# Split key, value and query weights of layer one stored by its second batch, cached rows written back from loaded tiles, and a new order of the work

## The chip, the cores and the metric

The kernel runs on one core of a Trainium2 chip. The metric is the device time of one launch in microseconds. Lower is better. Before the change the median of three runs is 2243.28 us (2240.95 to 2246.43).

## What is computed

Two layers of a streaming encoder on float32 data. There are 1024 frames of one new stream and 16 frames of each of eight running streams, 1152 rows of 1024 columns together. Each layer is a mixer and a gated convolution network, both added to the input:

```python
def trunk_layer(x, pos, cache_k, cache_v, ...):
    xn = rms_norm(x, norm_mix)
    q, k, v, u = mixer_inputs(xn, pos, w_in, q_gain, k_gain)     # xn @ w_in, 512 | 128 | 128 | 512 columns
    if cache_k is None:                                          # the new stream: a band of key chunks
        attn = window_attention_prompt(q, k, v, sinks); keys, vals = k, v
    else:                                                        # running streams: 128 cached keys and 16 new ones
        keys = jnp.concatenate([cache_k, k], axis=1); vals = jnp.concatenate([cache_v, v], axis=1)
        attn = sink_attention(q, keys, vals, sinks, None)
    pool, new_pool = pool_mixer(u, pool_prev, w_pool, pool_scale)
    x = x + jnp.concatenate([attn, pool], axis=-1) @ w_out
    f, new_conv = conv_ffn(rms_norm(x, norm_ffn), conv_prev, w_up, conv_w, conv_b, w_down)
    return x + f, keys[:, -WINDOW:], vals[:, -WINDOW:], new_pool, new_conv
```

The new cache of a running stream holds the 128 newest rows: rows 16 to 127 of the old cache, then the 16 new ones.

## The kernel before

**Tiles and batches.** The 1152 rows are nine tiles of 128 (tile 8 holds the running streams), in three batches of three tiles. A mixer works batch by batch. `n` streams normalise a batch and transpose it for TensorE. `k` units (12 in a batch) multiply it with the query, key and value columns of `w_in`, `u` units (8) with the pooling columns, `p` units (4) with the pooling weights, and `o` units (16) with `w_out`. A chain of steps named `L` prepares the heads and attends, tile after tile, in one fixed order. Then `m` streams normalise again, `s` units form the sums and differences of blocks for a Strassen product, and the up projection starts with units `v` (first half of the rows) and `w` (second half) on weights that `up_advance` loads and splits (`upw` does it ahead). The first up products are followed by a long regular stage (`up_units`), and that by the down projection in seven products (`down_units`, j from 0 to 6, with p counting the tiles of one product).

**Split weights.** A product is made of three matmuls on rounded parts (`mm3`): high by high, high by low, low by high. A piece of weights of 256 KB is loaded into a `raw` tile (5 buffers), ScalarE or VectorE rounds it into the high part, and VectorE subtracts to get the low part, both in one `W` tile (6 buffers, 512 KB). `w_split` (line 173) does this and, where the piece has a key, stores the split tile in DRAM (`wsd`, lines 187 to 189). A later unit with the same key finds it in `kept` and loads the split tile back with one 512 KB transfer (lines 178 to 180) and neither load nor split of its own. Three later splits and up to five later raw loads are written ahead of a unit (`w_advance`). So each mixer's first batch loads, splits and stores, and the second and third batches load the stored tiles. `keyed` (line 1359) gives the keys.

**The caches.** `sample` loads `cache_k` and `cache_v` of a layer as tiles of 128 partitions (cached row) by 8 streams by 128 (`load`, line 666; `loadv`, line 670). Rows 16 to 127 go to the output apart from that, DRAM to DRAM, in `copies` (line 1338), a unit that waits for nothing.

**Order.** Each unit is a `Token` with a key from `PLAN`: a stream has a first key and a step. `arrange` sorts by key and puts out the first unit whose predecessors are out and whose tiles have room. That is the order in which instructions are written. The framework then orders each queue again: instructions keep their written rank, and one that waits for nothing can be moved forward past others that do. All data transfers are issued by SyncE (SP), whose queue runs in order: a transfer that waits holds up those behind it. The DVE, ACT and PE queues run in order too.

**Other places the change touches.** `params1` (unit `par`) has 12 small transfers: two gains, the sinks nine times, and the pooling scale into a tile of the tag `D`. `xl1` loads the three input tiles of the second batch. `wt_load` (called in `down_units`, line 1221) loads six pieces of `w_down` into `W` tiles, one in each of p = 0 to 3 and two at p = 4 of the first down product; the third down product is the first to use them. Flags in `PLAN` (`e_...`) say for some copies whether VectorE (1) or ScalarE (0) makes them.

Of the kernel before, what the change touches and what calls it, by code (L numbers as in the profile page):

```python
# [44 lines left out]
def arrange(tokens, limits):  # L45
# [17 lines left out]


PLAN = [
    dict(k0=(-17.62, 0.24), u0=(10.61, 1.71), k1=(30.79, 2.26), u1=(78.0, 4.62), o0=(92.76, 2.89), k2=(148.67, 0.53), u2=(167.09, 2.77), o1=(177.0, 4.18), o2=(235.82, 4.28), p0=(40.1, 4.11), p1=(87.53, 9.52), p2=(194.05, 11.9), n1=(-17.77, 3.16), n2=(24.42, 3.62), n3=(92.75, 0.67), m0=(218.99, 3.57), m1=(259.62, 0.1), m2=(181.18, 1.22), d=(4.13, 4.36), L=(26.9, 49.72, 64.52, 85.1, 108.8, 144.29, 159.45, 183.94, 209.44, 245.41), cw=(276.93, 6.24), sc=(242.61, 32.45), s0=(252.65, 2.67), s1=(279.21, 6.7), v=(236.08, 0.18), w=(265.61, 1.32), upw=(297.57, 0.58), e_q=0, e_k=1, e_v=1, e_u=0, e_k2=0, e_qt=0, e_pt0=0, e_pt1=1, e_ps0=1, e_ps1=1, e_ks=0, e_w=1, e_x0=0, e_x1=0, e_x2=1),
    dict(k0=(-52.3, 0.11), u0=(39.12, 0.62), k1=(27.74, 4.1), u1=(77.36, 4.61), o0=(81.16, 2.69), k2=(144.54, 0.53), u2=(154.52, 4.44), o1=(176.58, 5.19), o2=(244.07, 2.25), p0=(50.25, 5.11), p1=(72.82, 0.77), p2=(195.1, 13.29), n1=(-13.38, 2.12), n2=(30.2, 4.39), n3=(93.86, 2.01), m0=(219.6, 1.94), m1=(237.49, 1.8), m2=(278.02, 1.14), d=(-26.81, 5.35), L=(26.9, 49.72, 64.52, 87.91, 107.72, 142.58, 160.43, 180.13, 216.19, 239.71), cw=(266.26, 12.19), sc=(271.63, 4.65), s0=(264.1, 2.05), s1=(266.18, 3.7), v=(283.58, 0.14), w=(284.07, 11.47), upw=(287.29, 0.87), e_q=1, e_k=1, e_v=0, e_u=1, e_k2=0, e_qt=0, e_pt0=0, e_pt1=0, e_ps0=1, e_ps1=1, e_ks=0, e_w=1, e_x0=0, e_x1=1, e_x2=0),
]


# [1 line left out]
def encoder_kernel(ctx: ExitStack, tc: tile.TileContext, consts, x_prompt, x_sample, cache_k, cache_v,  # L72
# [4 lines left out]
    pe, act, dve, pool, sync = nc.tensor, nc.scalar, nc.vector, nc.gpsimd, nc.sync  # L77
# [14 lines left out]
    def T(tag, shape, dt=F32):  # L92
        cnt[0] += 1
        n = 1
        for s in shape[1:]:
            n *= s
        assert n <= SIZE[tag], (tag, shape)
        t = sp.tile([128, SIZE[tag]], dt, tag=tag, name=f"{tag}{cnt[0]}", bufs=BUFS[tag])
        v = t[0:shape[0], 0:n]
        if len(shape) == 3:  # L100
            v = v.rearrange("p (a b) -> p a b", b=shape[2])
        elif len(shape) == 4:
            v = v.rearrange("p (a b c) -> p a b c", b=shape[2], c=shape[3])
        return v
# [556 lines left out]
    def sample(l):  # L661
        H = {}
# [3 lines left out]
        def load():  # L666
            H["ck"] = T("B", [128, 8, 128])
            sync.dma_start(out=H["ck"], in_=cache_k[l].rearrange("b t g d -> t b (g d)"))

        def loadv():  # L670
            H["cv"] = T("B", [128, 8, 128])
            sync.dma_start(out=H["cv"], in_=cache_v[l].rearrange("b t g d -> t b (g d)"))

        def kc(i):
            def f():
# [522 lines left out]
    def down_units(l):  # L1198
        us = []
        for u, (j, p) in enumerate(DSEQ):  # L1200
            n = 5 if j in (0, 1, 5, 6) else 4
            late = j == 5 and l < DEPTH - 1
            loads, splits = ((0, 2, 4, 5, 6), (0, 0, 2, 4, 5)) if n == 5 else ((0, 2, 4, 6), (0, 0, 2, 4))

            def f(u=u, j=j, p=p, n=n, late=late, loads=loads, splits=splits):
                if u == 0:
                    down_x(l, 0)
                if u + 2 < len(DSEQ):
                    g_load(l, u + 2)
                if u + 1 < len(DSEQ):  # L1210
                    down_x(l, u + 1)
                    g_split(l, u + 1)
                down_add(l, u, None)
                if j < 6 and not late:
                    for x in range(*(splits + (6,))[p:p + 2]):
                        wd_split(l, j + 1, x)
                    for x in range(*(loads + (6,))[p:p + 2]):
                        wd_load(l, j + 1, x)
                if j == 0:
                    for x in range(p, 6 if p == 4 else p + 1):  # L1220
                        wt_load(l, x)
# [12 lines left out]
            us.append(Unit(f))  # L1234
        return us

# [8 lines left out]
    def params1(l):  # L1245
        def f():
# [88 lines left out]
        x_load(0, [1, 2])()  # L1335
        sync.dma_start(out=cst[:, C_M:C_END], in_=consts[:, C_M:C_END])

    def copies(l):
        def f():
            sync.dma_start(out=nk_s[l, :, 0:112], in_=cache_k[l, :, 16:128])  # L1340
            sync.dma_start(out=nv_s[l, :, 0:112], in_=cache_v[l, :, 16:128])
        return f

    events = []
    pend = []
    for l in range(DEPTH):
# [9 lines left out]
                q = list((pre or {}).get(i, ())) + ([f"{st}.{i - 1}"] if i else [])  # L1356
                add(f"{st}.{i}", k + i * step, u, q, (res or {}).get(i))

        def keyed(x, units, l=l):
            for i, u in enumerate(units):  # L1360
                u.ws[0].key = l, x, i
            return units
# [24 lines left out]
            first = {3 if wd else 1: {"T6": 6}} if sn[0] == "n" else {}  # L1387
            stream(sn, norms(l, ts, sn[0], normB if sn[0] == "n" else normQ, wd), {0: npre[sn]}, first)
        add("spl", pl["u2"][0] - 20, spool_load(l), ["k1.11"])
        add("copy", pl["o1"][0], copies(l))  # L1390
        for b in range(3):
            nn = f"n{b + 1}.5"
            kres = {7: {"qkv": 3}, 11: {"V": 3}}
            stream(f"k{b}", keyed("k", kvq_units(l, b)), {0: [nn] + ([f"k{b - 1}.11"] if b else []), 11: ["par"]}, kres)
            stream(f"u{b}", keyed("u", u_units(l, b)), {0: [nn] + (["d.9"] if l else []), 3: [f"p{b - 1}.3"] if b else [], 7: [f"p{b}.0"] + (["spl"] if b == 2 else [])}, {7: {"T6": -6}})
# [14 lines left out]
            add(f"L.{i}", key, f, ([f"L.{i - 1}"] if i else ["par"] + (["d.9"] if l else [])) + list(pre), res)  # L1410
            lastidx[t] = i
        for b in range(3):
            ou = keyed("o", out_units(l, b))
# [93 lines left out]
```

## Time and profile before

| | |
|---|---|
| median of the runs | 2243.28 us |
| profiled execution, its own time | 2242.44 us |
| its span, first to last instruction | 2240.7 us |
| mean granted TensorE clock | 0.988 of 2.4 GHz |
| busy PE / DVE / ACT / POOL | 97% / 76% / 42% / 15% |
| chain that ended last: PE / DMA / DVE / ACT | 85% / 6% / 5% / 2% |
| moved by DMA | 389.64 MB, mean 174 GB/s |

The numbers come from one execution. The outside of the span is 1.7 us. A row of busy time says how long an engine had an instruction in work. Matmuls overlap, so their durations add up to more than the time they take; the starts of two neighbours give the real pace. The granted clock is 1.00 at 2.4 GHz and 0.5 at 1.2 GHz; a value between is a mean over a stretch with both. The mixer of layer one runs from 0 to about 405 us, its up projection to about 885 us, its down projection into layer two's mixer, which ends at about 1505 us; layer two's up projection ends at about 1985 us.

### The profile page before, as it was taken

What the parts mean: (1) busy time and instruction counts of PE and PEld (TensorE: products, weight loads), DVE (VectorE), ACT (ScalarE), POOL (GpSimd) and SP (SyncE); (2) the same over time, 40 slices, a digit from 0 to 9 for tenths busy, and PEclk for the clock granted to TensorE, in tenths of its full rate; (3) what the DMA queues carried; (4) which work ended last, traced back from release to release, by engine and by line L of the source; (5) the groups of instructions that cost most, each with busy time, mean ns of one, the idle gap of its engine ahead of it and who ended that gap; (6) DMA issues with size and microseconds to landing.
All of it is one profiled execution on the core that took longest, in us unless ns stands there. A gap on an engine that the chain in (4) does not pass through costs nothing.

```text
span 2240.7 us, 36002 instructions
## 1 busy us (share of the span) xinstructions
PE 2169.5 (97%) x13178; PEld 1945.5 (87%) x13178; DVE 1712.6 (76%) x3234; ACT 943.5 (42%) x1749; POOL 326.6 (15%) x499
## 2 busy tenths in 40 slices
PE   7999999899999999999999999979999999999999
PEld 6867777899999999878888887779999999988887
DVE  4776467989899998867557754689989999987663
ACT  3454345534343434443335543554343434353341
POOL 0000001121213232000000000111212233320000
PEclk9999999899999999999999999999999999999999
DMA  8757565122224346958765665532222343488663
GB/s 313 255 194 269 182 218 173 59 95 79 95 88 151 117 151 220 298 178 268 243 228 184 230 230 207 205 116 84 94 82 93 110 140 128 143 274 267 182 199 113
DMA packets 315940, 389.64 MB, mean 174 GB/s; under 512 B 21906, under 2 KB 219746, under 8 KB 315730
## 3 DMA queue, kind: packets, MB, share of 16 engines
q1 hardware_dynamic: 315762, 387.33, 52.2%
q8 instruction: 104, 1.70, 0.3%
q14 instruction: 74, 0.61, 0.1%
HBM read 279.71 MB, written 109.37 MB: 174 GB/s over the span
## 4 chain that ended last, share of the span: by engine, by line
PE 85%; DMA 6%; DVE 5%; ACT 2%; issue 1%; SPq 0%; POOL 0%; DVEq 0%; ACTq 0%
PE mm L154 15%; PE mm L155 15%; PE mm L156 15%; PE s L156 11%; PE s L154 11%; PE s L155 11%; PE s L644 2%; DMA raw<-in_w_down_dram 1%; DMA raw<-in_w_in_dram 1%; PE tr L631 1%; PE mm L448 1%; DMA W<-wd1o 1%; PE s L592 1%; DMA xd<-u 1%; PE tr L294 1%
## 5 line engine op out<-in xcount | busy, mean ns | idle before, releaser
L154 PE MATMUL mm<-B,W 128*128 128x288 f32 (+1 forms) x1376 | 422.1, 307 | 13.6 <-DVE B L927 7.7
L155 PE MATMUL mm<-B,W 128*128 128x288 f32 (+1 forms) x1376 | 419.2, 305 | 1.9 <-DVE B L315 1.8
L156 PE MATMUL mm<-B,W 128*128 128x288 f32 (+1 forms) x1376 | 417.2, 304 | 0.0
L154 PE MATMUL s<-B,B 128*128 128x512 f32 x704 | 279.6, 397 | 4.1 <-ACT B L1133 2.7
L156 PE MATMUL s<-B,B 128*128 128x512 f32 x704 | 279.2, 397 | 2.8 <-DVE B L1134 2.8
L155 PE MATMUL s<-B,B 128*128 128x512 f32 x704 | 278.6, 396 | 0.0
L154 PEld LDWEIGHTS mm<-B,W 128*128 128x128 f32 x1376 | 262.6, 191 | 17.9 <-DVE B L927 7.9
L155 PEld LDWEIGHTS mm<-B,W 128*128 128x128 f32 x1376 | 262.0, 190 | 3.4 <-DVE B L315 2.4
L156 PEld LDWEIGHTS mm<-B,W 128*128 128x128 f32 x1376 | 261.7, 190 | 1.0 <-DVE W L185 0.4
L975 DVE SCALAR_TENSOR_TENSOR B<-B,cvp,B 128x1168 f32<-128x1168 f32 x176 | 250.6, 1427 | 1.8 <-ACT B L973 1.5
L154 PE MATMUL mm<-W,B 128*128 128x512 f32 (+1 forms) x576 | 220.0, 388 | 12.4 <-ACT W L184 3.1
L155 PE MATMUL mm<-W,B 128*128 128x512 f32 (+1 forms) x576 | 214.8, 374 | 0.2 <-DVE W L185 0.2
L156 PE MATMUL mm<-W,B 128*128 128x512 f32 (+1 forms) x576 | 213.9, 374 | 0.0
L868 ACT CAST W<-Q 128x512 fp32r<-128x512 f32 x132 | 82.0, 621 | 258.1 <-PE mm L156 169.3
L1133 ACT CAST B<-B 128x256 fp32r<-128x256 f32 (+1 forms) x128 | 97.3, 780 | 204.7 <-DMA B<-gd 70.5
L154 PE MATMUL s<-B,W 128*128 128x288 f32 x576 | 171.2, 297 | 1.8 <-ACT B L314 1.2
L155 PE MATMUL s<-B,W 128*128 128x288 f32 x576 | 170.5, 296 | 0.0
L156 PE MATMUL s<-B,W 128*128 128x288 f32 x576 | 170.3, 296 | 0.0
L154 PEld LDWEIGHTS s<-B,B 128*128 128x128 f32 x704 | 133.2, 189 | 36.2 <-ACT B L1133 5.3
L156 PEld LDWEIGHTS s<-B,B 128*128 128x128 f32 x704 | 133.0, 189 | 34.9 <-DVE B L1134 3.6
L155 PEld LDWEIGHTS s<-B,B 128*128 128x128 f32 x704 | 133.1, 189 | 30.7
L869 DVE TENSOR_TENSOR W<-Q,W 128x512 fp32r<-128x512 f32 x132 | 134.6, 1020 | 20.6 <-ACT W L868 20.6
(236 smaller groups left out, 4855.8 us busy)
## 6 DMA issues: line engine op xcount, KB each, us to landing
raw<-in_w_up_dram SPq DMA_DIRECT2D x176, 256.0 KB
raw<-in_w_down_dram SPq DMA_DIRECT2D x154, 256.0 KB
gd<-B SPq DMA_DIRECT2D x44, 576.0 KB
B<-gd SPq DMA_DIRECT2D x32, 576.0 KB
W<-wd0o SPq DMA_DIRECT2D x32, 512.0 KB
W<-wd1o SPq DMA_DIRECT2D x32, 512.0 KB
W<-wd0k SPq DMA_DIRECT2D x24, 512.0 KB
W<-wd1k SPq DMA_DIRECT2D x24, 512.0 KB
```

What stands on the lines that cost most here:

```text
L154: pe.matmul(out=out, lhsT=a[0], rhs=b[0], start=first, stop=False)
L155: pe.matmul(out=out, lhsT=a[0], rhs=b[1], start=False, stop=False)
L156: pe.matmul(out=out, lhsT=a[1], rhs=b[0], start=False, stop=last)
L294: pe.transpose(out=tr[:, k * 128:(k + 1) * 128], in_=xn[:, c:c + 128], identity=ident)
L448: pe.matmul(out=o, lhsT=w.raw, rhs=d, start=True, stop=True)
L592: pe.matmul(out=p[:, i, kr], lhsT=q[:, h], rhs=K[:, g, kr], start=True, stop=False)
L631: pe.transpose(out=tr[:, h * 128:(h + 1) * 128], in_=S[:, h, kk * 128:(kk + 1) * 128], identity=ident)
L644: pe.matmul(out=o, lhsT=V, rhs=H.pop(("p", g, kk)), start=kk == kks[0], stop=kk == 1)
L868: act.copy(out=hi, in_=src)
L869: dve.tensor_tensor(out=lo, in0=src, in1=f32(hi), op=ALU.subtract)
L975: dve.scalar_tensor_tensor(out=c, in0=h[:, j:j + 1168], scalar=cvp[:, j, ct:ct + 1], in1=c, op0=ALU.mult, op1=ALU.add)
L1133: act.copy(out=h, in_=f32(o))
```

## The change

1. The first batch of layer one no longer gives keys to its 12 `k` pieces, so it loads and splits them and does not store them. The second batch loads the raw pieces and splits them again, and stores them. The third loads the stored ones, as before. Layer two and the `u` and `o` pieces stay as they were.
2. `copies` is gone. `load` and `loadv` each get a second transfer that writes rows 16 to 127 from the tile just loaded to the output.
3. `wt_load` is called for no piece at p = 0 and 1, for two each at p = 2, 3 and 4.
4. The pooling scale's tile takes the tag `V` instead of `D`.
5. The keys of nearly all streams are new, and some flags. In layer one `e_w`, `e_k` and `e_pt1` become 0 and `e_u` and `e_k2` become 1; in layer two `e_q`, `e_k` and `e_u` become 0 and `e_v` becomes 1.

What the keys do to the written order, in the places that matter below. Layer one: `xl1` and `par` move from behind `k0.10` to before `k0.0`; `n2` and the first head steps are written between the `u0` units and not behind them; four `u2` units come before the running streams' steps; the first products' `upw` and the `s1` units: before, `upw` was written ahead of `o2.15` and the `s1` units between the `w` units, and now `upw` comes last and all `s1` units before `w.0`. The eight small loads of the convolution state (`scl`) move from behind `o2.1` to before `o1.13`. Layer two: the units `v.0` to `v.3` are written between `m2.0` and `m2.1`; before they came after `m2.4` and `m2.5`.

```diff
 PLAN = [
-    dict(k0=(-17.62, 0.24), u0=(10.61, 1.71), ... n1=(-17.77, 3.16), n2=(24.42, 3.62), ... sc=(242.61, 32.45), ... v=(236.08, 0.18), w=(265.61, 1.32), upw=(297.57, 0.58), e_q=0, e_k=1, e_v=1, e_u=0, e_k2=0, ... e_pt1=1, ... e_w=1, ...),
-    dict(k0=(-52.3, 0.11), ... m2=(278.02, 1.14), ... v=(283.58, 0.14), w=(284.07, 11.47), upw=(287.29, 0.87), e_q=1, e_k=1, e_v=0, e_u=1, ...),
+    dict(k0=(12.35, 0.15), u0=(27.6, 1.13), ... n1=(-86.25, 2.26), n2=(26.8, 3.63), ... sc=(227.68, 60.94), ... v=(209.05, 0.65), w=(316.25, 1.16), upw=(342.36, 0.16), e_q=0, e_k=0, e_v=1, e_u=1, e_k2=1, ... e_pt1=0, ... e_w=0, ...),
+    dict(k0=(-43.86, 0.15), ... m2=(278.02, 1.14), ... v=(278.27, 0.1), w=(272.47, 516.37), upw=(298.18, 0.41), e_q=0, e_k=0, e_v=1, e_u=0, ...),
 ]
...
             sync.dma_start(out=H["ck"], in_=cache_k[l].rearrange("b t g d -> t b (g d)"))
+            sync.dma_start(out=nk_s[l, :, 0:112].rearrange("b t g d -> t b (g d)"), in_=H["ck"][16:128])
...
             sync.dma_start(out=H["cv"], in_=cache_v[l].rearrange("b t g d -> t b (g d)"))
+            sync.dma_start(out=nv_s[l, :, 0:112].rearrange("b t g d -> t b (g d)"), in_=H["cv"][16:128])
...
                 if j == 0:
-                    for x in range(p, 6 if p == 4 else p + 1):
+                    for x in range(max(2 * p - 4, 0), max(2 * p - 2, 0)):
                         wt_load(l, x)
...
-            r = T("D", [4, 128])
+            r = T("V", [4, 128])
...
-    def copies(l):
-        def f():
-            sync.dma_start(out=nk_s[l, :, 0:112], in_=cache_k[l, :, 16:128])
-            sync.dma_start(out=nv_s[l, :, 0:112], in_=cache_v[l, :, 16:128])
-        return f
-
...
-        def keyed(x, units, l=l):
+        def keyed(x, units, b, l=l):
+            if l == 0 and x == "k" and b == 0:
+                return units
             for i, u in enumerate(units):
                 u.ws[0].key = l, x, i
             return units
...
-        add("copy", pl["o1"][0], copies(l))
```

## Rows read from the trace of the kernel before

**Rows 1.** Busy time of each engine: us, share of the span, instructions.
```profile
PE 2169.5 (97%) x13178; PEld 1945.5 (87%) x13178; DVE 1712.6 (76%) x3234; ACT 943.5 (42%) x1749; POOL 326.6 (15%) x499
```
**Rows 2.** Stages: start:end, length, busy us (instructions) by engine, granted clock, DMA share, GB/s.
```profile
40.00:50.00 10.00, 7.44 (x42) 7.03 (x41) 4.18 (x11) 2.06 (x4) 0.00 (x0) 0.83 0.95 347
55.00:65.00 10.00, 6.98 (x34) 6.04 (x33) 8.66 (x23) 3.88 (x9) 0.71 (x2) 0.83 0.82 310
140.00:160.00 20.00, 15.39 (x65) 9.57 (x63) 12.93 (x50) 10.32 (x31) 1.39 (x2) 0.83 0.40 140
385.00:410.00 25.00, 18.26 (x96) 16.02 (x95) 22.47 (x27) 13.04 (x19) 3.28 (x6) 0.74 0.04 11
880.00:900.00 20.00, 17.70 (x88) 14.67 (x87) 15.64 (x24) 8.81 (x13) 2.46 (x5) 0.91 1.10 356
1480.00:1510.00 30.00, 18.68 (x116) 17.03 (x115) 27.40 (x33) 16.89 (x25) 7.47 (x7) 0.83 0.18 61
1980.00:2000.00 20.00, 16.79 (x87) 14.16 (x86) 15.58 (x25) 9.03 (x12) 1.90 (x4) 0.91 1.08 352
```
**Rows 3.** PE in order of time: start, us, line, tiles, idle before and its releaser.
```profile
43.65 0.51 PE L154 MATMUL mm<-W,B 128*128 128x256 f32 x2 [2.34 <-ACT W L184]
...
59.52 1.54 PE L278 MATMUL tr<-cst,B 128*128 128x128 f32 x6 [3.02 <-DVE B L258]
```
**Rows 4.** Chain that ended last, 0 to 60 us: start, us, what.
```profile
4.72 8.47 DMA raw<-in_w_in_dram
...
24.45 7.16 DMA wd0k<-W
31.63 4.83 DMA raw<-in_w_in_dram
```
**Rows 5.** SP's queue in order of time, first 50 us.
```profile
4.72 2.85 SPq L218 DMA_DIRECT2D raw<-in_w_in_dram  x3
...
14.41 5.97 SPq L1254 DMA_DIRECT2D snk<-in_attn_sinks_dram  x7
...
22.60 0.81 SPq L1340 DMA_DIRECT2D out_dram<-in_cache_k_dram  x1
...
28.50 0.63 SPq L1340 DMA_DIRECT2D out_dram<-in_cache_k_dram  x1
...
44.21 2.30 SPq L247 DMA_DIRECT2D B<-in_x_prompt_dram  x3
```
**Rows 6.** DMA issues of the whole run: count and size of each.
```profile
W<-wd0k SPq DMA_DIRECT2D x24, 512.0 KB
...
wd0k<-W SPq DMA_DIRECT2D x12, 512.0 KB
...
out_dram<-in_cache_k_dram SPq DMA_DIRECT2D x2, 448.0 KB
```
**Rows 7.** From the chain: an up weight piece landing, and a 512 KB load.
```profile
399.56 2.89 DMA raw<-in_w_up_dram
...
1387.95 7.04 DMA B<-xd
```
**Rows 8.** The third split of the run and a later one: ACT, then DVE.
```profile
13.31 0.62 ACT L184 CAST W<-raw 128x512 fp32r<-128x512 f32 x1
...
43.63 0.69 DVE L185 TENSOR_TENSOR W<-raw,W 128x512 fp32r<-128x512 f32 x1 [7.94 <-ACT W L184]
```
**Rows 9.** Busy time by engine while the second batch is worked on.
```profile
60.00:160.00 100.00, 94.56 (x508) 76.70 (x507) 69.33 (x246) 51.16 (x141) 8.16 (x6) 0.95 0.60 211
```
**Rows 10.** SP's queue around the cache loads of layer one.
```profile
222.97 0.39 SPq L668 DMA_DIRECT2D B<-in_cache_k_dram  x1
231.91 1.04 SPq L179 DMA_DIRECT2D W<-wd0u  x2
...
247.99 0.43 SPq L672 DMA_DIRECT2D B<-in_cache_v_dram  x1
250.94 0.33 SPq L179 DMA_DIRECT2D W<-wd0o  x1
```
**Rows 11.** PE's longest wait behind the start: us in total, times, longest.
```profile
PE mm L154 <- DVE B L927: 7.7, 1, 7.7
```
**Rows 12.** Into the down projection: SP's queue, then the chain.
```profile
866.64 3.58 SPq L1068 DMA_DIRECT2D W<-in_w_down_dram  x2
870.31 1.99 SPq L1078 DMA_DIRECT2D raw<-in_w_down_dram  x3
...
871.44 12.21 DMA raw<-in_w_down_dram x2
```

More of the change, by code (lines that the diff above doesn't have):

```diff
@@ L65 @@
 PLAN = [
-    dict(k0=(-17.62, 0.24), u0=(10.61, 1.71), k1=(30.79, 2.26), u1=(78.0, 4.62), o0=(92.76, 2.89), k2=(148.67, 0.53), u2=(167.09, 2.77), o1=(177.0, 4.18), o2=(235.82, 4.28), p0=(40.1, 4.11), p1=(87.53, 9.52), p2=(194.05, 11.9), n1=(-17.77, 3.16), n2=(24.42, 3.62), n3=(92.75, 0.67), m0=(218.99, 3.57), m1=(259.62, 0.1), m2=(181.18, 1.22), d=(4.13, 4.36), L=(26.9, 49.72, 64.52, 85.1, 108.8, 144.29, 159.45, 183.94, 209.44, 245.41), cw=(276.93, 6.24), sc=(242.61, 32.45), s0=(252.65, 2.67), s1=(279.21, 6.7), v=(236.08, 0.18), w=(265.61, 1.32), upw=(297.57, 0.58), e_q=0, e_k=1, e_v=1, e_u=0, e_k2=0, e_qt=0, e_pt0=0, e_pt1=1, e_ps0=1, e_ps1=1, e_ks=0, e_w=1, e_x0=0, e_x1=0, e_x2=1),
@@ L67 @@
-    dict(k0=(-52.3, 0.11), u0=(39.12, 0.62), k1=(27.74, 4.1), u1=(77.36, 4.61), o0=(81.16, 2.69), k2=(144.54, 0.53), u2=(154.52, 4.44), o1=(176.58, 5.19), o2=(244.07, 2.25), p0=(50.25, 5.11), p1=(72.82, 0.77), p2=(195.1, 13.29), n1=(-13.38, 2.12), n2=(30.2, 4.39), n3=(93.86, 2.01), m0=(219.6, 1.94), m1=(237.49, 1.8), m2=(278.02, 1.14), d=(-26.81, 5.35), L=(26.9, 49.72, 64.52, 87.91, 107.72, 142.58, 160.43, 180.13, 216.19, 239.71), cw=(266.26, 12.19), sc=(271.63, 4.65), s0=(264.1, 2.05), s1=(266.18, 3.7), v=(283.58, 0.14), w=(284.07, 11.47), upw=(287.29, 0.87), e_q=1, e_k=1, e_v=0, e_u=1, e_k2=0, e_qt=0, e_pt0=0, e_pt1=0, e_ps0=1, e_ps1=1, e_ks=0, e_w=1, e_x0=0, e_x1=1, e_x2=0),
+    dict(k0=(12.35, 0.15), u0=(27.6, 1.13), k1=(35.46, 2.26), u1=(78.0, 4.62), o0=(92.76, 2.89), k2=(160.39, 1.54), u2=(167.47, 3.15), o1=(177.0, 4.09), o2=(235.74, 4.2), p0=(40.1, 3.5), p1=(86.68, 12.45), p2=(194.05, 11.9), n1=(-86.25, 2.26), n2=(26.8, 3.63), n3=(92.6, 1.1), m0=(218.99, 3.57), m1=(260.89, 0.13), m2=(181.58, 0.95), d=(-13.48, 3.86), L=(26.9, 49.72, 64.52, 85.45, 108.8, 144.29, 158.38, 183.7, 209.44, 245.41), cw=(259.88, 23.53), sc=(227.68, 60.94), s0=(257.44, 3.18), s1=(268.93, 2.61), v=(209.05, 0.65), w=(316.25, 1.16), upw=(342.36, 0.16), e_q=0, e_k=0, e_v=1, e_u=1, e_k2=1, e_qt=0, e_pt0=0, e_pt1=0, e_ps0=1, e_ps1=1, e_ks=0, e_w=0, e_x0=1, e_x1=0, e_x2=0),
@@ new lines @@
+    dict(k0=(-43.86, 0.15), u0=(49.49, 0.1), k1=(26.26, 4.1), u1=(76.32, 4.61), o0=(81.16, 2.69), k2=(139.16, 1.11), u2=(150.18, 5.15), o1=(175.45, 5.19), o2=(244.07, 2.25), p0=(49.92, 3.56), p1=(56.81, 4.29), p2=(193.02, 12.48), n1=(-18.93, 0.85), n2=(30.53, 4.46), n3=(92.15, 1.8), m0=(222.0, 1.72), m1=(234.28, 0.33), m2=(278.02, 1.14), d=(-24.93, 3.08), L=(26.9, 49.72, 64.52, 87.91, 106.15, 148.52, 158.51, 180.13, 216.19, 239.71), cw=(264.41, 12.12), sc=(273.99, 6.32), s0=(264.1, 2.08), s1=(276.75, 4.45), v=(278.27, 0.1), w=(272.47, 516.37), upw=(298.18, 0.41), e_q=0, e_k=0, e_v=1, e_u=0, e_k2=0, e_qt=0, e_pt0=0, e_pt1=0, e_ps0=1, e_ps1=1, e_ks=0, e_w=1, e_x0=0, e_x1=1, e_x2=0),
@@ L1393, in encoder_kernel @@
             kres = {7: {"qkv": 3}, 11: {"V": 3}}
-            stream(f"k{b}", keyed("k", kvq_units(l, b)), {0: [nn] + ([f"k{b - 1}.11"] if b else []), 11: ["par"]}, kres)
-            stream(f"u{b}", keyed("u", u_units(l, b)), {0: [nn] + (["d.9"] if l else []), 3: [f"p{b - 1}.3"] if b else [], 7: [f"p{b}.0"] + (["spl"] if b == 2 else [])}, {7: {"T6": -6}})
+            stream(f"k{b}", keyed("k", kvq_units(l, b), b), {0: [nn] + ([f"k{b - 1}.11"] if b else []), 11: ["par"]}, kres)
+            stream(f"u{b}", keyed("u", u_units(l, b), b), {0: [nn] + (["d.9"] if l else []), 3: [f"p{b - 1}.3"] if b else [], 7: [f"p{b}.0"] + (["spl"] if b == 2 else [])}, {7: {"T6": -6}})
             if b == 2:
@@ L1412, in encoder_kernel @@
         for b in range(3):
-            ou = keyed("o", out_units(l, b))
+            ou = keyed("o", out_units(l, b), b)
             pre = {0: [f"p{b}.3"], 4: [f"L.{lastidx[3 * b + 2]}"]}
```

## The prediction

> **What bounds the kernel now.** I read the share of each engine first, then the stages, then PE's waits, then the chain, then SP's queue. PE is busy for 2169.5 us [rows 1] of a span of 2240.7, so 71.2 us are left in which it has nothing to do, and what a new order can win is there or in the slow clock behind it. The stages show where. A loss is counted as idle time plus (1 - granted clock) times length, an upper figure, because some slow clock falls into the idle time. The loss is 2.56 + 1.70 = 4.3 us at 40 to 50, 3.02 + 1.70 = 4.7 at 55 to 65, 4.61 + 3.40 = 8.0 at 140 to 160, 6.74 + 6.50 = 13.2 at 385 to 410, 2.30 + 1.80 = 4.1 at 880 to 900, 11.32 + 5.10 = 16.4 at 1480 to 1510, and 3.21 + 1.80 = 5.0 at 1980 to 2000 [rows 2]. Everything else is PE at its own pace, with the same matmuls before and after.
>
> In the first 65 us the cause is the traffic. PE waits 2.34 us for a rounding on ACT and then 3.02 us for the second batch's normalisation [rows 3]. Followed back, the first wait is a store of a split weight (7.16 us) that had to leave its W tile, and behind it a raw load (4.83 us) [rows 4]. DMA is 95% busy there at 347 GB/s [rows 2]. The second wait is of the same origin: the input tiles of the second batch are issued at 44.21 us, in the middle of that traffic [rows 5].
>
> **The change, part by part.** All sums are made against the profiled execution's 2242.44 us (span 2240.7 and 1.7 outside it), which lies 0.84 us under the median of the runs, so nothing is converted.
>
> *Stores out of the first batch, copies away, inputs earlier.* Twelve stores of 512 KB [rows 6] leave the first 50 us, 6.3 MB or 18 us at 347 GB/s. The copies of both layers, four of 448 KB [rows 6], were written far behind, yet they were issued from 22.60 to about 30 us [rows 5]: a transfer that waits for nothing is moved to wherever SP is free. They leave too, 1.8 MB or 5.3 us. The three input tiles come in ahead (1.5 MB, 4.5 us). The first wait loses its cause, and the second one as well, because the inputs are asked for some 30 us earlier. Bounds: 0 to 4.3 and 0 to 4.7. I take all of both, -9.0. What is late next is PE itself, or the head steps on DVE.
>
> *Twelve small transfers ahead of the raw loads.* `par` is now written before `k0.0`, and its transfers wait for nothing. Seven of them took 5.97 us of SP, 0.85 each [rows 5], so twelve take up to 10.2 us, and the three raw loads that SP issued at 4.72 go out at about 15. Landing takes between 2.89 us [rows 7] and 8.47 [rows 4], so the third split comes at 18 to 23 us and not at 13.31 [rows 8]. Meanwhile PE has two pieces (18 matmuls) and 24 transposes. Bounds 0 to 5 us; +1.5, nearer to the low end because that cover stands in front and the stores are no longer beside these loads.
>
> *The second batch splits twelve pieces.* Twelve casts on ACT at 0.62 and twelve subtractions on DVE at 0.69 [rows 8] make 7.4 and 8.3 us. Twelve stored tiles are no longer read there (the 24 reads [rows 6] become 12), but twelve raw loads and twelve stores come: per piece 768 KB in place of 512. From 60 to 160 us DVE is busy 69.33 of 100 and ACT 51.16, PE 94.56 and DMA 60% [rows 9]. So there is room in the sum: 30 us of DVE for 8.3, and 40% of DMA for 3.1 MB more. It is not free on the queues, which run in order: a subtraction waits for its cast and the cast for its load, and the head steps of tiles 0 to 3 stand behind them. Bounds 0 to 8.3 (all twelve on the path); +2.5, about the 30% for which DVE is idle, taken off from the lower side. Should that cover go, it costs the 8.3.
>
> *Cached rows written from the tile.* Each of the four new stores waits on SP until its load has landed. A 512 KB load took 7.04 us [rows 7]. Behind the key load SP has nothing to issue for 8.94 us, which hides it; behind the value load the next weight load follows after 2.95 us [rows 10], so it would be held for 4.1 us, in either layer. The split tiles already loaded ahead cover most of that. Bounds 0 to 8.2; +1.0.
>
> *Ends of the mixers.* In layer two PE's longest wait behind the start, 7.7 us, is for a DVE sum behind which splits and normalisation were queued [rows 11], and the stretch loses 16.4 us. Now `v.0` to `v.3` and with them the first up weights stand before the last tiles' normalisation, so PE has work while that runs. Bounds -9 to +4 (the wait and its clock, or the 3.2 by which the two layers' ends differ, the other way round); -4.5, about half. In layer one it is the reverse: the units that prepare these weights move from ahead of `o2.15` to `v.0`, behind `m2`, which is how layer two was. Its 13.2 could become 16.4. Bounds -4 to +9; +1.0, because the weights' loads are free to move forward anyway.
>
> *w_down pieces later.* SP issues two 512 KB pieces at 866.64, before three raw loads at 870.31, and the raw loads take 12.21 us to land, on the chain [rows 12]. If the pieces really go later, the 4.1 and 5.0 us of the two transitions shrink. But they wait for nothing but a free tile, so like the copies they may be issued just as early. Bounds 0 to -6; -2.0.
>
> *The rest.* Flags move copies between DVE and ACT in both directions, the scale's tile has another tag, and the third batch has its units in another order. PE covers these, since it is the bound there; 0, with 4 either way. The 8.0 us at 140 to 160, where PE has run out of work that does not wait for the heads, I leave as they are.
>
> Sum: -9.0 + 1.5 + 2.5 + 1.0 - 4.5 + 1.0 - 2.0 = -9.5, so 2242.44 - 9.5 = 2232.9, or **2233 us**.
>
> **The rivals.**
> - *Given back in the second batch* (2242 us). The head steps set the end of the second batch, not PE: at 140 to 160 PE idles for want of them [rows 2]. If the 8.3 us of subtractions fall on them in full, the 9.0 are gone, and the other terms are too small to show: 2242.44 - 9.0 + 8.3 = 2241.7. For it: that idle stretch. Against it: the head steps begin earlier as well, by as much as the first batch ends earlier.
> - *More than forecast* (2222 us). The splits hide wholly (-2.5), layer two's end gives its full 9 (-4.5), and the earlier heads halve the 8.0 (-4.0): 2232.9 - 11.0 = 2221.9. For it: DVE's 30 free us [rows 9]. Against it: three things have to go well.
> - *SP is held by the cached rows* (2240 us). A store that waits 7.04 us [rows 7] stands in front of the weights that PE needs next, 4.1 us late for either value tile, and nothing loaded ahead covers it: the term is 8.2 and not 1.0, 2232.9 + 7.2 = 2240.1. For it: the 2.95 us in which SP issues the next load [rows 10]. Against it: three later splits are loaded ahead. The Trainium skill (DMA: Bandwidth & Descriptors, "Two DMAs through the same engine are not ordered") says that the engine which issues a transfer needing another's data has to wait for the first one's completion. No row here shows a store right behind the load of its own tile, so whether SP stands still for it is open.
> - *The stall moves with the stores* (2254 us, slower). The second batch now has what starved the first: raw load, split and store in a row, with the store keeping its W tile for 7.16 us [rows 4]. If the raw loads again land after 8.47 us and not 2.89, PE stalls twice there as it did (9.0 us), and the in-order DVE queue, blocked as for 7.94 us in the first batch [rows 8], keeps the head steps waiting by the whole 8.3. Then -9.0 + 9.0 + 8.3 + 1.5 + 1.0 + 1.0 with nothing from the last two gains: 2254.2. It decides where DMA in the second batch passes from 60% to the 95% of the first. Against it: the twelve pieces of the second batch are spread over some 100 us [rows 9], those of the first over less than half of that.
> - *The keys do not reach the queues.* Transfers that wait for nothing go where SP is free, whatever their key. That would take back the -2.0 alone, and is inside the forecast.
>
> **How the numbers follow.** Forecast 0.40, more than forecast 0.17, given back 0.20, SP held 0.06, the stall moves 0.17. About what a measurement of this kernel can tell from no change is 0.3%, 6.7 us: faster is under 2236.6, slower over 2250.0. The forecast's own range is 2226 to 2240; its upper end gives 0.02 to no difference. Faster 0.40 + 0.17 - 0.02 = 0.55, same 0.20 + 0.06 + 0.02 = 0.28, slower 0.17. The range reaches to 2218 (the larger gain and the 4 us of the rest) and to 2253, just short of the slower case.
>
> **What would show it.** Right: DMA's first 50 us no longer at 95%, no store of `wd0k` before about 60 us, PE's waits of 2.34 and 3.02 us gone and the clock at 1.00 through 40 to 65; the second batch's DVE about 8 us busier; less than 12 us lost at layer two's end. Wrong in a step: a PE wait before 25 us for a split (the small transfers), SP idle for over 4 us in front of a weight load just behind a cache load, w_down pieces still ahead of the raw loads. The whole is wrong if the idle stretch before 160 us grows by what the first 65 us lose.

## The result, and the profile after

The changed kernel takes 2230.26 us (median of 7 runs, 2228.70 to 2237.58) against 2244.48 us for the kernel before on the same chip (7 runs, 2239.06 to 2246.46). The ratio is 0.9947 with a 95% interval of 0.9931 to 0.9963, that is 11.9 us faster, with 8.3 to 15.5 us as bounds (the two medians lie 14.2 us apart). The profiled execution took 2230.1 us (span 2228.3) against 2242.44.

PE's idle time has gone from 71.2 us [rows 1] to 67.8 us. The page's row of the changed kernel (us, share of the span, instructions):

```profile
PE 2160.5 (97%) x13178; PEld 1938.4 (87%) x13178; DVE 1707.7 (77%) x3210; ACT 966.8 (43%) x1797; POOL 325.7 (15%) x499
```

PE's own busy time fell by 9.0 us with the same number of matmuls. So of the 12.4 us by which the span is shorter, 3.4 are idle time and 9.0 are busy time. The mean granted clock is 0.995 in this execution (0.992 to 0.995 in the seven), before it was 0.988; that is up to 15.6 us over the span, a part of which falls into idle time. Now the stages of the changed kernel, columns as in [rows 2]. The last four windows are moved back by as much as their stage now comes earlier, 10.5 to 13.9 us.

```profile
40.00:50.00 10.00, 10.00 (x76) 10.00 (x76) 7.02 (x15) 4.09 (x10) 2.51 (x2) 1.00 0.89 311
55.00:65.00 10.00, 10.00 (x62) 9.60 (x61) 8.64 (x23) 3.92 (x7) 0.00 (x0) 1.00 1.00 362
140.00:160.00 20.00, 17.59 (x90) 12.95 (x89) 14.77 (x52) 13.85 (x40) 1.95 (x1) 1.00 0.63 221
...
374.50:399.50 25.00, 18.64 (x98) 16.43 (x98) 23.96 (x28) 13.69 (x20) 4.23 (x7) 0.80 0.04 11
866.50:886.50 20.00, 18.17 (x97) 15.09 (x97) 16.27 (x26) 9.17 (x13) 3.46 (x6) 1.00 1.10 360
1467.40:1497.40 30.00, 21.11 (x126) 18.55 (x124) 25.86 (x31) 17.11 (x28) 6.09 (x6) 0.85 0.15 47
1966.10:1986.10 20.00, 17.87 (x94) 15.23 (x94) 16.82 (x27) 9.04 (x12) 2.74 (x8) 0.91 1.08 361
```

Counted as in the prediction (idle plus the slow clock's share), the losses of [rows 2] went from 4.3 to 0, from 4.7 to 0, from 8.0 to 2.4, from 13.2 to 11.4, from 4.1 to 1.8, from 16.4 to 13.4, and from 5.0 to 3.9. The two waits of [rows 3] are gone.

Where the lead is won and lost is seen from the start times of a few lines (us earlier than before): the first attention score 6.4, the last transposes of layer one's third batch 5.8, the end of its second normalisation 11.4, its first convolution 10.5, its down projection 13.5, layer two's first normalisation 14.5, its first convolution 12.6, its down projection 13.9, the end of the span 12.4. So the gain is made in layer one, and mostly in two places: before the first score (6.4), and between the third batch's last transposes and the end of the second normalisation (5.6). Between the first score and those transposes nothing is won. These two stretches show it, columns as in [rows 2], before and then changed; counted as above they lose 9.1 and 14.6 us before, and 8.8 and 7.3 after the change:

```profile
72.40:209.10 136.70, 130.34 (x686) 104.56 (x683) 102.96 (x340) 71.94 (x198) 12.21 (x9) 0.98 0.65 228
209.10:391.80 182.70, 173.63 (x944) 139.91 (x941) 107.73 (x266) 81.47 (x213) 14.94 (x16) 0.97 0.59 197
```

```profile
66.00:203.30 137.30, 128.54 (x682) 103.53 (x681) 105.80 (x343) 77.90 (x210) 14.04 (x10) 1.00 0.66 229
203.30:380.40 177.10, 169.80 (x943) 137.49 (x941) 101.24 (x254) 85.78 (x221) 14.55 (x16) 1.00 0.61 209
```

What layer two shows (14.5 down to 12.4) is within what its length scatters between kernels that have the same layer two: from its first normalisation to the end of the span, 1131.7 to 1141.7 us in the five that have the new keys for it, 1134.9 of them in the changed kernel.

SP's queue of the changed kernel in order of time (start, us, line, transfer, count) shows the order the change meant: small transfers, raw pieces, inputs, raw pieces, and no store of `wd0k` in the first 50 us.

```profile
8.94 5.60 SPq L1256 DMA_DIRECT2D snk<-in_attn_sinks_dram  x8
14.58 0.36 SPq L1258 DMA_DIRECT2D V<-in_pool_scale_dram  x1
14.99 2.25 SPq L218 DMA_DIRECT2D raw<-in_w_in_dram  x5
17.29 1.39 SPq L247 DMA_DIRECT2D B<-in_x_prompt_dram  x3
19.17 16.70 SPq L218 DMA_DIRECT2D raw<-in_w_in_dram  x10
```

While the second batch is worked on, DVE is busier than in [rows 9] by 5.0 us and ACT by 6.7, and PE less by 2.4. The same window of the changed kernel:

```profile
60.00:160.00 100.00, 92.19 (x505) 75.12 (x504) 74.31 (x252) 57.82 (x158) 10.39 (x6) 1.00 0.64 222
```

Around the cache loads of layer one, SP's queue of the changed kernel. The stores (L669, L674) are issued 8.30 and 4.77 us behind their loads, and for 5.5 and 4.3 us ahead of them the queue issues nothing. Below the queue stand its own waits there (us in total, times, longest): they end with the landing of those loads.

```profile
224.28 0.45 SPq L668 DMA_DIRECT2D B<-in_cache_k_dram  x1
224.97 1.65 SPq L179 DMA_DIRECT2D W<-wd0o  x1
226.72 0.38 SPq L179 DMA_DIRECT2D W<-wd0k  x1
232.58 0.35 SPq L669 DMA_DIRECT2D out_dram<-B  x1
...
253.62 0.43 SPq L673 DMA_DIRECT2D B<-in_cache_v_dram  x1
258.39 0.35 SPq L674 DMA_DIRECT2D out_dram<-B  x1
```

```profile
SPq L669 <- DMA B<-in_cache_k_dram: 5.4, 1, 5.4
SPq L674 <- DMA B<-in_cache_v_dram: 4.3, 1, 4.3
```

### The profile page after: what moved, and what is told of

It reads as the page before. It is cut to its first block, busy times and chain, and to the rows that moved or that the text cites. A ratio compares the mean times of both kernels' runs of the same rounds, so it can differ in the third digit from the quotient of the medians.

```text
span 2228.3 us, 36072 instructions
## 1 busy us (share of the span) xinstructions
PE 2160.5 (97%) x13178; PEld 1938.4 (87%) x13178; DVE 1707.7 (77%) x3210; ACT 966.8 (43%) x1797; POOL 325.7 (15%) x499
## 4 chain that ended last, share of the span: by engine, by line
PE 80%; DMA 9%; DVE 6%; ACT 2%; issue 1%; SPq 1%; DVEq 0%; POOL 0%; ACTq 0%
PE mm L154 15%; PE mm L156 14%; PE mm L155 14%; PE s L154 10%; PE s L156 10%; PE s L155 10%; PE s L644 2%; DMA raw<-in_w_down_dram 2%; DMA B<-gd 1%; DMA W<-wd0o 1%; DMA u<-xd 1%; PE tr L631 1%; DMA out_dram<-u 1%; PE s L592 1%; PE mm L448 1%
## 5 line engine op out<-in xcount | busy, mean ns | idle before, releaser
L154 PE MATMUL mm<-B,W 128*128 128x288 f32 (+1 forms) x1376 | 421.7, 306 | 12.5 <-ACT B L314 10.4
L154 PE MATMUL mm<-W,B 128*128 128x512 f32 (+1 forms) x576 | 216.6, 382 | 10.9 <-ACT B L281 2.8
```

What stands on the lines that cost most here:

```text
L154: pe.matmul(out=out, lhsT=a[0], rhs=b[0], start=first, stop=False)
```

## The experiments

The question was which part brings the gain: the early traffic that is gone (stores and copies), the inputs asked for earlier, or the new order. "The skipped stores" below are the first edit of the title: layer one's first batch stores no key, value and query weights, and the second batch splits them again. Every run below was timed in five rounds beside the kernel before, and a ratio is to that kernel in the same rounds. Line numbers behind line 670 are 2 higher where the copies are gone. The edits are shown in short. What is read from a trace is one execution of each kernel.

### Undoing one part of the changed kernel

**The first batch stores again.** The skipped stores undone, all else as changed.

```diff
-            if l == 0 and x == "k" and b == 0:
-                return units
```

> The changed kernel, but layer one's first batch stores its twelve split pieces again and the second batch reads them; keys, cached rows and all else as changed. Theory (the stores starved the first 65 us): DMA back at over 90% before 50 us, a PE wait of 2 to 4 us for a split between 30 and 60 us, the first scores 3 to 6 us later, and 2234 to 2238 us, since the second batch gets back 2 to 4 us of its splits. Rival (the new keys did it, the stores were hidden by the earlier input loads): first scores within 1.5 us of the changed kernel's 66.0 and 2226 to 2231 us, as twelve splits fall away.

Measured 2225.87 us, ratio 0.9926 (0.9910 to 0.9942). That is lower than the changed kernel, but the intervals overlap. The stores do not stop PE: at 20 to 60 us DMA is full and PE is never idle. Stages of this kernel:

```profile
20.00:40.00 20.00, 20.00 (x107) 16.65 (x106) 8.32 (x16) 10.05 (x21) 0.52 (x1) 1.00 1.03 380
40.00:60.00 20.00, 20.00 (x137) 19.90 (x136) 15.96 (x40) 8.90 (x21) 2.37 (x2) 1.00 0.97 374
```

**The copies are back**, and the stores from the cache tiles gone.

```diff
-            sync.dma_start(out=nk_s[l, :, 0:112]..., in_=H["ck"][16:128])
-            sync.dma_start(out=nv_s[l, :, 0:112]..., in_=H["cv"][16:128])
+        add("copy", pl["o1"][0], copies(l))
```

> The changed kernel, but rows 16 to 127 of the caches are copied DRAM to DRAM again by a unit that waits for nothing, with the same key as before; nothing is written from the loaded tiles. Theory (the copies are issued in the first 50 us and cost DMA time there, now less crowded): they are issued between 15 and 50 us, the first scores come 0 to 2 us later, and the whole is 2230 to 2233 us. Rival (the stores from the tiles hold SP behind the cache loads, so taking them away wins): 2224 to 2228 us, with the weight loads behind the value load 3 to 4 us earlier.

Measured 2229.14 us, 0.9944 (0.9930 to 0.9959): no difference from the changed kernel. The copies are again issued early, from 17.52 to about 27.5 us. With the stores out of the first batch, they cost nothing that can be measured.

**The old keys and flags**, both layers.

```diff
-PLAN = [new, new]
+PLAN = [old, old]
```

> The changed kernel with both layers' old keys and flags: only the parts are new (no stores in the first batch, cached rows from tiles, later w_down pieces, the scale's tile). Theory (the gain is made in the first 65 us by the stores that left): the first scores at 66 to 69 us and 2234 to 2238 us, about half of the 14 us. Rival (the keys carry it, and the parts alone lose by the twelve splits): 2241 to 2247 us.

Measured 2235.70 us, 0.9972 (0.9962 to 0.9981). About half of the gain goes with the keys; the interval just touches that of the changed kernel. Its span is 6.3 us longer (2234.6 and 2228.3). The changed kernel is ahead of it by 2.6 us at the third batch's last transposes and by 6.8 us at the end of the second normalisation, so most of what the keys win is won between these two.

**The small transfers behind `k0.10`**, where they were.

```diff
-        add("par", 10, params1(0))
+        add("par", 13.95, params1(0))
```

> The changed kernel with the unit of the twelve small transfers written behind k0.10 and not before k0.0; the three input loads stay ahead. Theory (the small transfers delay the third raw load by 10 us and cost PE 1.5 to 3 us before 25 us): raw loads three to five issued at about 5 us and not 15, PE's wait before 25 us gone, first scores 1 to 3 us earlier, 2227 to 2230 us. Rival (PE has other work until then, nothing is lost): the same first scores and 2230 us.

Measured 2229.59 us, 0.9943 (0.9928 to 0.9959). PE is idle for 1.7 us less in the first 65 us (12.29 and not 14.02) and the first score comes 3.2 us earlier, but the first convolution comes 0.4 us later than in the changed kernel: the lead is not kept.

**Layer two with its old keys.**

```diff
-    PLAN[1] = new
+    PLAN[1] = old
```

> The changed kernel with layer two's old keys and flags. In the changed kernel layer two's mixer, from its first transposes to its first convolution, took 413.1 us against 411.2 before, though its end lost less. Theory (layer two's new keys bring nothing and cost about 2 us): 2226 to 2230 us, that stretch at 411 to 412 us, and the wait of 7 to 8 us for a DVE sum near its end is back. Rival (the earlier v units gain and something else hides it): 2232 to 2236 us.

Measured 2230.40 us, 0.9950 (0.9932 to 0.9968): layer two's new keys bring nothing that can be measured. PE's waits from 1400 to 1520 us (us in total, times, longest) show why. First the changed kernel, then this one:

```profile
PE mm L154 <- ACT B L314: 6.8, 4, 3.9
PE mm L154 <- DMA W<-wd1o: 1.6, 1, 1.6
PE mm L155 <- DVE B L315: 1.5, 2, 1.4
```

```profile
PE mm L154 <- DVE B L929: 7.7, 1, 7.7
PE mm L154 <- ACT B L314: 1.3, 1, 1.3
```

The 7.7 us for a DVE sum [rows 11] have become 6.8 us for ACT's copies of the normalised tiles.

### One part alone, on the kernel before

**Only the stores left out of the first batch** (old keys, copies as before).

```diff
+            if l == 0 and x == "k" and b == 0:
+                return units
```

> The kernel before with one edit: layer one's first batch stores no key, value and query pieces, the second batch splits and stores them. Theory (the stores starved the first 65 us, and the splits cost the second batch about 4 us): PE's wait of 2.34 us before 44 us gone, the first scores at 68 to 70 us, then 3 to 5 us lost between 60 and 100 us, in all 2238 to 2242 us. Rival (the stores were never the cause): first scores at 71 to 73 us and 2244 to 2249 us, the splits being pure loss.

Measured 2235.78 us, 0.9982 (0.9971 to 0.9993). The skipped stores alone are worth 4.0 us.

**Only the cached rows from the tiles**, no copies.

```diff
+            sync.dma_start(out=nk_s[l, :, 0:112]..., in_=H["ck"][16:128])
+            sync.dma_start(out=nv_s[l, :, 0:112]..., in_=H["cv"][16:128])
-        add("copy", pl["o1"][0], copies(l))
```

> The kernel before with one edit: the cached rows are written from the loaded tiles, and the DRAM to DRAM copies are gone. Theory (the four copies, issued from 22.60 to 30 us, are a large part of what held the store and the raw load behind PE's wait at 41 us): that wait shrinks to under 1 us, first scores 1.5 to 4 us earlier than 72.4, 2238 to 2242 us. Rival (the stores alone are enough to starve it): the wait stays, first scores within 1 us, 2241 to 2245 us.

Measured 2228.29 us, 0.9941 (0.9924 to 0.9959): as much as the whole change, with all the stores still in the first batch. Stages of this kernel, to be held against [rows 2]:

```profile
40.00:50.00 10.00, 10.00 (x69) 10.00 (x68) 6.04 (x16) 2.69 (x6) 2.48 (x2) 1.00 1.03 379
50.00:60.00 10.00, 10.00 (x62) 9.65 (x61) 9.25 (x27) 4.31 (x10) 0.00 (x0) 1.00 1.03 399
```

Both stalls are gone although DMA moves more than before. The copies (1.8 MB at 22 to 30 us) had stood between the raw pieces and their stores; without them the second batch's inputs went out at 38.51 us, before at 44.21 [rows 5]. Whether it is the copies' place in the queue or their bytes that made the first stall, this run does not separate.

**Only the inputs early.**

```diff
-            add("xl1", 8, x_load(0, [3, 4, 5]), ["n1.5"])
+            add("xl1", -18, x_load(0, [3, 4, 5]), ["n1.5"])
```

> The kernel before with one key changed: the second batch's three input loads are written before k0.0 and not behind k0.10. Theory (PE's 3.02 us wait at 56 to 60 us is for inputs asked for too late): that wait is gone, first scores 2 to 5 us earlier, while the first wait at 41 us stays or grows by up to 2 us since the input loads add 1.5 MB to the crowded start: 2237 to 2242 us. Rival (the crowding decides, not the place in the queue): the waits only move, first scores within 1 us of 72.4, 2242 to 2246 us.

Measured 2231.17 us, 0.9951 (0.9933 to 0.9969). Here only the second stall goes. The first one stays, as the same stages show:

```profile
40.00:50.00 10.00, 6.16 (x36) 5.50 (x35) 4.96 (x10) 2.29 (x6) 0.28 (x1) 0.76 0.92 349
50.00:60.00 10.00, 10.00 (x56) 9.96 (x55) 7.59 (x23) 3.24 (x8) 2.33 (x1) 0.90 0.96 349
```

That does not explain the whole ratio: this execution is 3.0 us ahead of the kernel before at the third batch's last transposes and 10.9 us at the end. Most of its lead comes later, and what makes it there stays open.

### Putting parts together

**Cached rows from the tiles, and the stores left out** (old keys).

```diff
+            if l == 0 and x == "k" and b == 0:
+                return units
...
+            sync.dma_start(out=nk_s[l, :, 0:112]..., in_=H["ck"][16:128])
-        add("copy", pl["o1"][0], copies(l))
```

> The kernel before, with the cached rows from the tiles and without the first batch's stores of key, value and query weights (the second batch splits them again and stores them); old keys. Theory: once the copies are gone the first batch's stores no longer stop TensorE, so leaving them out wins nothing and the second batch's twelve splits cost what was taken at 2.5 us: 2 to 5 us slower than the cached rows alone, ratio 0.995 to 0.996 of before; TensorE's idle time at 60 to 160 us grows from 6.4 us by as much. Rival: leaving out the stores wins by itself, as the 4.3 us of the run with that edit alone would have it, and the two add up: 0.992.

Measured 2234.68 us, 0.9976 (0.9967 to 0.9986). The interval lies wholly above that of the cached rows alone: leaving out the stores makes that kernel slower, by about 8 us. The theory's direction holds, its size (2 to 5 us) does not.

**Cached rows from the tiles, and the inputs early** (old keys).

```diff
-            add("xl1", 8, x_load(0, [3, 4, 5]), ["n1.5"])
+            add("xl1", -18, x_load(0, [3, 4, 5]), ["n1.5"])
...
+            sync.dma_start(out=nk_s[l, :, 0:112]..., in_=H["ck"][16:128])
-        add("copy", pl["o1"][0], copies(l))
```

> The kernel before, with the cached rows from the tiles and the second batch's three input tiles asked for ahead of the first piece; old keys otherwise. Theory: each of the two edits alone (ratios 0.9941 and 0.9951) removes the same early stalls, so that together they give hardly more than the larger: 0.993 to 0.9945. Rival: they take away different waits and add up, 0.9941 - 0.0049 = 0.989 to 0.990.

Measured 2232.95 us, 0.9968 (0.9956 to 0.9979): neither more than the larger of the two, nor the sum, and the median is above either alone. The intervals overlap (with the cached rows alone just so), so that the two together are slower is not shown; that they do not add up is. In the two profiled executions the clock differs behind the start. Stages of this kernel, and then of the cached rows alone:

```profile
100.00:140.00 40.00, 36.10 (x185) 29.24 (x184) 29.99 (x108) 20.03 (x59) 3.93 (x2) 0.95 0.62 214
140.00:160.00 20.00, 18.18 (x87) 13.39 (x86) 12.89 (x45) 11.36 (x33) 2.26 (x2) 0.93 0.40 130
```

```profile
100.00:140.00 40.00, 35.90 (x191) 28.84 (x190) 29.64 (x105) 20.89 (x61) 3.92 (x2) 1.00 0.61 214
140.00:160.00 20.00, 18.88 (x100) 15.13 (x99) 16.78 (x56) 13.24 (x38) 2.51 (x2) 1.00 0.53 184
```

PE's idle time is 5.7 against 5.2 us; the slow clock takes 0.05 x 40 + 0.07 x 20 = 3.4 us more. Together that is 3.9 us, and the third batch's last transposes come 3.9 us later (201.5 and 197.6 us). Why the clock fell in one and not in the other with nearly the same idle time stays open, and so does whether it makes the difference between the kernels: over all their runs the mean clocks are alike (0.990 to 0.994 here, 0.988 to 0.992 with the cached rows alone), and the two spans differ by 8.2 us, more than this stretch explains.

**Cached rows from the tiles, and the keys for layer one's end.** Of the new plan it has `o2`, `m0` to `m2`, `cw`, `sc`, `s0`, `s1`, `v`, `w`, `upw` and `e_w`.

```diff
-    dict(... o2=(235.82, 4.28), ... cw=(276.93, 6.24), sc=(242.61, 32.45), ... upw=(297.57, 0.58), ...)
+    dict(... o2=(235.74, 4.2), ... cw=(259.88, 23.53), sc=(227.68, 60.94), ... upw=(342.36, 0.16), ...)
...
+            sync.dma_start(out=nk_s[l, :, 0:112]..., in_=H["ck"][16:128])
-        add("copy", pl["o1"][0], copies(l))
```

> The kernel before, with the cached rows written from the loaded tiles (no copies), and of layer one's new keys only those for the end of the mixer (o2, m0 to m2, cw, sc, s0, s1, v, w, upw and the flag e_w). Theory: the unpredicted part of the changed kernel's gain, 4.7 us between the last batch's normalisation and the first convolution (208.5 us before, 203.8 after), comes from these keys alone. The stretch, 206.1 us with the cached rows alone, falls to about 203 to 204, and the time goes 2 to 5 us below that of the cached rows alone (ratio 0.9941): 0.992 to 0.993 of before. Rival: the stretch depends on the state in which the rest of the new keys leaves the queues, and these keys do nothing by themselves, or what the reference of layer one's end said in the prediction (+1.0, up to +9): the stretch stays at 206 or grows to 210, ratio 0.994 to 0.998.

Measured 2230.09 us, 0.9953 (0.9941 to 0.9965); from the last transposes of the third batch to the first convolution it takes 206.8 us (206.1 with the cached rows alone). The theory fell: these keys bring nothing by themselves.

**The first batch stores again, and the small transfers are late** (new keys).

```diff
-            if l == 0 and x == "k" and b == 0:
-                return units
-        add("par", 10, params1(0))
+        add("par", 13.95, params1(0))
```

> The changed kernel with the first batch storing its key, value and query weights again, as before the change, and with the twelve small transfers (par) again behind k0.10. Theory: both undo costs of the start (first score 3.9 us and 3.2 us earlier in the runs that undid one of them), but the two share one cover, the empty TensorE before 25 us, and what is early at the first score is mostly spent by the end of the mixer (1.0 us and -0.4 us were left there): about the time of the run that stores in the first batch, ratio 0.992 to 0.9935. Rival: the two add up and stay, first score at 59 us and a ratio of 0.990 to 0.991.

Measured 2228.71 us, 0.9951 (0.9938 to 0.9963). It has the earliest first convolution of all (402.7 us; 407.1 in the changed kernel) and is not the fastest. Its lead over the changed kernel goes in layer two, in which the two kernels are the same (1141.7 and 1134.9 us in one execution each).

No version is shown to beat the changed kernel: the lowest ratio, 0.9926, overlaps with 0.9947.

### What the runs say together

PE's share of two stretches, 0 to 65 and 65 to 160 us, tells what the skipped stores do. Three pairs, each with the stores in the first batch and then without them. The kernel before, and with the skipped stores alone:

```profile
0.00:65.00 65.00, 47.50 (x242) 41.17 (x243) 32.07 (x74) 22.92 (x45) 4.81 (x10) 0.95 0.85 311
65.00:160.00 95.00, 89.56 (x486) 72.31 (x484) 64.33 (x230) 48.24 (x134) 8.16 (x6) 0.96 0.59 209
```

```profile
0.00:65.00 65.00, 52.54 (x286) 45.99 (x287) 39.22 (x93) 26.81 (x53) 4.85 (x10) 1.00 0.81 288
65.00:160.00 95.00, 85.32 (x449) 67.73 (x448) 68.56 (x235) 51.42 (x143) 9.76 (x6) 0.95 0.57 201
```

The cached rows from the tiles, and with the skipped stores too:

```profile
0.00:65.00 65.00, 52.06 (x297) 46.57 (x298) 37.85 (x91) 28.08 (x56) 5.36 (x11) 1.00 0.92 340
65.00:160.00 95.00, 89.09 (x489) 72.51 (x488) 69.84 (x249) 50.96 (x145) 9.97 (x6) 1.00 0.58 206
```

```profile
0.00:65.00 65.00, 52.56 (x292) 46.70 (x293) 40.52 (x97) 27.53 (x54) 4.85 (x10) 1.00 0.78 273
65.00:160.00 95.00, 84.67 (x452) 66.74 (x451) 68.72 (x235) 52.69 (x147) 9.81 (x6) 0.96 0.56 195
```

The changed kernel with the stores back in the first batch, and the changed kernel:

```profile
0.00:65.00 65.00, 50.99 (x291) 45.56 (x292) 36.79 (x92) 29.69 (x62) 4.85 (x10) 1.00 0.88 319
65.00:160.00 95.00, 89.44 (x491) 72.70 (x490) 68.40 (x233) 51.36 (x148) 9.73 (x7) 1.00 0.64 220
```

```profile
0.00:65.00 65.00, 50.98 (x283) 45.01 (x284) 39.07 (x84) 30.79 (x60) 4.47 (x10) 1.00 0.77 263
65.00:160.00 95.00, 87.19 (x477) 70.45 (x475) 70.62 (x243) 55.51 (x154) 10.39 (x6) 1.00 0.63 215
```

In the first stretch skipping the stores saves 5.0 us of idle time (and the slow clock) beside the copies and the late inputs, and 0.5 and 0.0 us where these are gone. In the second it costs 4.2, 4.4 and 2.3 us of idle time, always, and in the middle pair the clock falls from 1.00 to 0.96 too, 3.8 us more, which together is the 8 us of that pair. So in this change skipping the stores is no gain: what it cures was already removed by another part.

The keys of layer one are the second part that counts, but the runs show it only where the stores are skipped. There the ratio is 0.9976 or 0.9972 with the old keys and 0.9947 with the new ones. Where the first batch stores, it is 0.9941 with the old keys (the cached rows alone) and 0.9926 with the new ones, which can't be told apart. So the cached rows alone are as fast as the whole change: the skipped stores take about 8 us of that gain away, and the new keys bring about 6 back.

One wait goes with the old keys. In all eight kernels that have the old ones for the batches, PE waits 2.7 us in one piece for L621, a head step on DVE, between 100 and 165 us; in none of the six with the new ones does it wait for that line there. PE in order of time (idle before and its releaser in brackets), the kernel before, and behind it the longest wait of the changed kernel from 130 to 165 us:

```profile
143.53 1.35 PE L631 MATMUL tr<-cst,B 128*128 128x128 f32 x8 [2.68 <-DVE B L621]
146.35 0.69 PE L556 MATMUL tr<-cst,ks 128*128 128x128 f32 x2 [1.47 <-ACT PT L151]
```

```profile
141.94 0.65 PE L556 MATMUL tr<-cst,ks 128*128 128x128 f32 x4 [1.25 <-ACT PT L151]
```

This is not where the lead grows: from the first score to the third batch's last transposes the changed kernel takes 137.3 us and the kernel before 136.7, since idle time that went from this place came back ahead of it (from 60 to 100 us PE is idle for 5.1 us, before for 0.7). From the third batch's last transposes to the first convolution the six kernels with the new keys take 203.5 to 206.7 us, the eight others 206.1 to 209.6. Which of the keys does it was not tried, beyond those of the end.

## Why the prediction was right, point by point

The time (2233 forecast, 2230.26 measured) and the direction were right, and so was the likeliest mechanism for the start. The parts are not all of the size that they were given, and that the total is within 3 us is partly luck: the 6.5 us of two gains did not come as told, and some 5.6 us came where the sum had nothing.

- *Stores, copies, inputs, -9.0.* The size is right: the stages of 4.3 and 4.7 us now lose nothing. The cause was told too one-sidedly. I weighed the parts by their bytes, 18 us of stores against 5.3 of copies. The runs show that either of these is enough (the cached rows alone, the stores alone), and that the DMA's share does not tell: it stood at 1.03 in the run without copies, with PE never idle from 40 to 60 us. The second stall goes by the queue's order alone (only the inputs early); for the first, order and bytes are not separated.
- *Twelve small transfers, +1.5.* Right in size: 1.7 us of PE's idle time, though the first score comes 3.2 us later for it. The raw pieces went out at 14.99 us (forecast about 15) and the third was rounded at 17.80 (forecast 18 to 23). The run that put them back shows that this cost is then absorbed elsewhere.
- *The second batch's splits, +2.5.* Right: 2.3 us of PE's idle time in the changed kernel. DVE was busier by 5.0 us and not by about 8. With the old keys it is 4.2 to 4.4 us, and on the cached rows 3.8 more of slow clock: 8.2, all of the 8.3 of the rival that gives the gain back. That rival did not hold here, and did hold on the cached rows with the old keys.
- *Cached rows, +1.0.* The wait is real, the cost is not. SP stood still ahead of each store: the one of the value tile went out 4.77 us behind its load, where the forecast took 7.04. PE's waits for `wd0o` between 200 and 320 us come to 2.3 us in both kernels, so the pieces loaded ahead cover it. This settles what was open about the rule of the Trainium skill (DMA: Bandwidth & Descriptors, "Two DMAs through the same engine are not ordered"): the trace agrees that the issuing engine waits for the first transfer.
- *Layer two's end, -4.5.* This step failed. "PE has work while that runs" was true for one wait and made another: 6.8 us for ACT in place of 7.7 us for DVE. The stretch loses 3.0 us less (13.4, and not under 12 as the sign of being right had it), but the kernel with the old keys for layer two is as fast.
- *Layer one's end, +1.0.* Nearly nothing, as forecast: 0.9 us more from the end of the second normalisation to the first convolution, though the stage itself loses 1.8 less.
- *w_down later, -2.0.* The two transitions shrank by 2.3 and 1.1 us, but not for that reason: the pieces did not go later. In layer one the first went out 27.2 us ahead of the down projection's first split, before 28.0, and two still went ahead of the three raw loads, as SP's queue of the changed kernel shows:

```profile
853.88 3.56 SPq L1070 DMA_DIRECT2D W<-in_w_down_dram  x2
857.53 1.47 SPq L1080 DMA_DIRECT2D raw<-in_w_down_dram  x3
```

  So the rival that the keys do not reach the queues holds for this part. Nor do the runs show a gain: the kernel with the old keys differs from the one with cached rows and skipped stores by this edit and the scale's tag alone, and their ratios are 0.9972 and 0.9976. What shrank the transitions stays open.
- *The stage at 140 to 160 us*, left at 8.0, fell to 2.4, but this is a gain of the window more than of the kernel: idle time moved ahead of it. From 60 to 160 us, where the splits also fall, the loss went from 10.4 to 7.8 ([rows 9] and the same window above).
- *"Everything else is PE at its own pace"* was wrong, and with it the 0 for *the rest*. From 209.1 to 391.8 us the kernel before lost 14.6 us, nearly all of it ahead of the stage at 385; the changed kernel loses 7.3 in the same work. This is the largest gain that the sum did not have, and it covers for the two that failed.

The gain of the changed kernel is thus the early stalls (9.0, less the 1.7 and 2.3 paid for them) and what the new keys of layer one win, most of it behind the third batch's last transposes. Which of the keys does that, and through which wait, stays open. The wait for L621 is no answer: the run with the cached rows alone has it, keeps the full clock there and is as fast.

## What to carry to other kernels

Where a queue is full and PE waits, several transfers can each be the one too many: take each away alone before paying for the removal of the largest, because here 1.8 MB of copies were worth as much as a whole change and taking out 6.3 MB of stores, once these were gone, cost time. Gains that remove the same stall do not add up, so what a part costs must be tried on the kernel that has the other parts. A loss that a window no longer shows may have moved: compare stretches that hold the same work. A stall that goes by reordering at the end of a stage is to be followed to the next wait in the same stage before it is counted.

## What was not expected of the hardware

DMA's share of 95% with a stalled PE looked like a limit and was not one: the kernel without the copies moved 389 GB/s from 40 to 60 us (372 before) and PE was busy throughout. And the clock fell in one stretch and not in another with almost the same idle time (3.90 and 1.82 us at a clock of 0.95 and 0.93, 4.10 and 1.12 at 1.00), which is 3.4 us between two executions.
